# Diagonal of a 2-D prefix sum: engines in program order, six loads queued, the last groups cut in pieces, the last rows folded

## Chip, cores, metric

One core of a Trainium2 chip. The metric is device time in microseconds (us). The profile's span, from the first to the last instruction, is mostly 1.7 to 2 us shorter than the time (in a few runs up to 3.5). In profile lines PE is TensorE, PEld its weight loads, DVE VectorE, ACT ScalarE, POOL GpSimd and SP SyncE (a q behind it is the engine's queue), and L312 is line 312 of the run's kernel.

## The reference

```python
def reference(x):                       # x: float32, (4, 4224, 4224)
    ps = np.cumsum(np.cumsum(x, axis=1), axis=2)
    diag = np.diagonal(ps, axis1=1, axis2=2)
    return np.cumsum(diag, axis=1).astype(np.float32)      # (4, 4224)
```

Element i of the diagonal of `ps` is the sum of the square x[0..i, 0..i]. Its step from i-1 to i is row i left of and on the diagonal plus column i above it. So only row sums up to the diagonal and column sums above it are needed, and then two scans.

## The kernel before

A matrix is cut into 11 groups of 384 rows (3 rows on each of 128 partitions). A group is one DMA that also casts to bf16. TensorE adds the columns right of the group's diagonal block with a vector of ones into one row of `d` in PSUM. VectorE makes the masked diagonal block (`mu`) and, together with ScalarE (`act_sum`), the row sums. At a matrix's end the row sums are transposed into `d` by a matmul with the identity, and two scans run along the 11 rows.

```python
    strips = ctx.enter_context(tc.tile_pool(name="strips", bufs=6))
    ...
    head = last.tile([P, HEAD], FP32, name="head")           # the last 128 rows' last 1056 columns
    nc.sync.dma_start(out=head, in_=x[LB, TB:N, N - HEAD : N])
    ...
    prefetched = {(0, g): load_group(0, g) for g in range(2)}
    ...                                                      # constants
        for g in range(ng):                                  # ng = 11, in the last matrix 10
            strip = prefetched.pop((b, g), None)
            if strip is None:
                strip = load_group(b, g)
            ws = scalar_cols(g)
            for q in range(F):
                nc.vector.scalar_tensor_tensor(out=mu, in0=strip[:, q, lo:hi], ..., accum_out=ru[:, g, q : q + 1])
                columns(g, 0, GW, mu)
                if ws > 0:
                    act_sum(sa[:, g, q : q + 1], strip[:, q, :ws])
            nc.vector.reduce_sum(out=rs[:, g, :], in_=strip[:, :, ws:hi], axis=AX.X)
            for j in range(g + 1, NG):
                for q in range(F):
                    columns(j, 0, GW, strip[:, q, j * GW : (j + 1) * GW])
        ...                                # rows = rs + sa - ru, identity matmuls, scans, carries, y, store
```

In the last matrix the eleventh group is treated apart: 256 rows as pairs (`strip`, four DMAs) and the last 128 rows (`tail`, three DMAs). Their sums follow the scans in the text, but the tile scheduler orders every engine's instructions, so the text's order is not the executed one.

## Time and profile before

| | before |
|---|---|
| time, median of 3 | 674.47 us (674.30 to 674.58) |
| span | 672.8 us |
| bytes read from HBM | 285.47 MB, the input once |
| last full group (group 9 of the last matrix) starts to be worked on | 649.3 us |
| last piece of data landed | 663.3 us |
| final store issued | 670.8 us |

The table is read from its end: between the last data and the end lie 9.5 us, and before that the transfers set the pace. I call the moment when the engines start on the last data of group 9 "L9" all through the text. A strip is the tile of one group, a piece a range of its columns that is loaded by its own DMA, and a crossing is the time from the end of an instruction on one engine to the start of the next on another.

### The profile page before, as it was taken

Reading aid. Unit: us, or ns where it says so; the run is one execution under the profiler, and the core shown is the slowest. Engines: PE = TensorE matmul, PEld = TensorE weight load, DVE = VectorE, ACT = ScalarE, POOL = GpSimd, SP = SyncE. Lnnn points to the kernel's source line nnn. Section 1 sums busy time; section 2 is a strip of 40 time slices with the busy share of each in tenths; the row PEclk is TensorE's granted clock in tenths of the full one; section 3 lists DMA queues with packets and bytes.
Section 4 is the critical chain, followed back from the end, with each engine's and each line's share of the span. In section 5 each row is a group of like instructions: output and inputs, shape, how many; then the busy total and the mean of one; then the engine's idle time right before and its main releaser. Section 6 shows DMA issues by size and latency. Waiting matters only on the chain.

```text
span 672.8 us, 2608 instructions
## 1 busy us (share of the span) xinstructions
PE 232.5 (35%) x852; PEld 91.2 (14%) x852; DVE 259.3 (39%) x370; ACT 153.9 (23%) x249; POOL 31.8 (5%) x67
## 2 busy tenths in 40 slices
PE   0073453211155543321116543232204534344213
PEld 0031111000022211100002211110001211111001
DVE  2033333344543223334563222334555222234458
ACT  0011222233301112223420111223440011123342
POOL 3010000000000000000000000000000000100000
PEclk9997766555577766566557766766555776766655
DMA  9999999999999999999999999999999999999994
GB/s 202 217 215 218 217 217 217 217 217 217 217 219 217 217 218 217 217 217 217 217 217 218 218 217 217 217 215 217 218 217 217 217 217 218 217 217 217 217 201 76
DMA packets 7958, 143.23 MB, mean 213 GB/s; under 512 B 861, under 2 KB 1546, under 8 KB 2442
## 3 DMA queue, kind: packets, MB, share of 16 engines
q0 software_dynamic: 7712, 142.47, 99.0%
q1 hardware_dynamic: 234, 0.61, 0.3%
q8 instruction: 6, 0.10, 0.1%
q14 instruction: 6, 0.05, 0.0%
HBM read 285.47 MB, written 0.07 MB: 424 GB/s over the span
## 4 chain that ended last, share of the span: by engine, by line
another core or an unknown queue 51%; DVE 36%; DMA 11%; issue 1%; POOL 0%; PE 0%; DVEq 0%; POOLq 0%
DVE rs L252 24%; DMA strip<-in_x_dram 11%; DVE mu L240 9%; DVE lrs L334 1%; DVE c L198 1%; DVE c L190 1%; DVE y L281 0%; DVE y L273 0%; DVE tsum L362 0%; POOL strip L60 0%; DVE lc L190 0%; DVE lc L198 0%; PE d_last L156 0%; DVEq L240 0%
## 5 line engine op out<-in xcount | busy, mean ns | idle before, releaser
L165 ACT ACTIVATE dump<-strip 128x192 bf16<-128x192 bf16 (+11 forms) x124 | 141.1, 1138 | 507.7 <-DMA strip<-in_x_dram 505.1
L240 DVE SCALAR_TENSOR_TENSOR mu<-strip,um 128x384 bf16<-128x384 bf16 x129 | 65.5, 554 | 380.9 <-DMA strip<-in_x_dram 380.9
L252 DVE TENSOR_REDUCE rs<-strip 128x3 f32<-128x1152 bf16 (+10 forms) x43 | 169.8, 3950 | 27.5 <-DMA strip<-in_x_dram 27.5
L156 PE MATMUL d<-mu,sel 128*11 128x384 bf16 x129 | 59.2, 476 | 318.8 <-DVE mu L240 318.5
L156 PE MATMUL d<-strip,sel 128*11 128x384 bf16 x630 | 161.9, 431 | 0.0
L156 PEld LDWEIGHTS <-sel 128*11 128x11 bf16 (+1 forms) x794 | 86.7, 109 | 538.8 <-issue 515.2
L60 POOL DMA_DIRECT2D strip<-in_x_dram x43 | 23.0, 535 | 507.5 <-PE d L156 256.7
L156 PE MATMUL d_last<-strip,sel 128*1 128x384 bf16 (+1 forms) x32 | 14.2, 477 | 84.8 <-DMA strip<-in_x_dram 84.8
L165 ACT ACTIVATION_READ_ACCUMULATOR dump<-strip 128x1 f32 x124 | 23.1, 186 | 0.0
L156 PE MATMUL d<-ident,rows 128*11 128x128 f32 (+1 forms) x24 | 5.8, 415 | 19.9 <-DVE sa L219 13.2
L240 DVE DVE_READ_ACCUMULATOR mu<-strip,um 128x1 f32 x129 | 10.5, 82 | 0.0
L156 PEld LDWEIGHTS d<-ident,rows 128*11 128x11 f32 (+1 forms) x24 | 2.7, 128 | 24.0 <-DVE sa L219 15.0
L156 PE MATMUL fin<-wtri,tsum 128*1 128x128 f32 x8 | 2.4, 401 | 6.7 <-DVE tsum L362 3.9
L334 DVE TENSOR_REDUCE lrs<-strip 128x2 f32<-128x1664 bf16 (+2 forms) x3 | 4.4, 1459 | 0.0
L198 DVE TENSOR_TENSOR_SCAN c<-ones_row,c 11x384 f32<-11x384 f32 (+1 forms) x4 | 3.8, 940 | 0.0
L190 DVE TENSOR_TENSOR_SCAN c<-ones_row,d 11x384 f32<-11x384 f32 (+1 forms) x4 | 3.7, 935 | 0.0
L308 POOL DMA_DIRECT2D strip<-in_x_dram x3 | 1.6, 538 | 43.1 <-DMA strip<-in_x_dram 28.5
L362 DVE TENSOR_REDUCE tsum<-strip 128x1 f32<-128x792 bf16 (+2 forms) x3 | 2.9, 952 | 0.0
L156 PE MATMUL d_last<-mu,sel 128*1 128x256 bf16 x2 | 0.8, 396 | 5.5 <-DVE mu L316 5.5
L304 POOL DMA_DIRECT2D strip<-in_x_dram x3 | 2.1, 708 | 6.7 <-DMA strip<-in_x_dram 6.7
L82 POOL TENSOR_SCALAR_AFFINE_SELECT um<-um 128x384 bf16<-128x384 bf16 (+2 forms) x6 | 2.4, 434 | 0.1
L281 DVE TENSOR_TENSOR y<-y,c 11x384 f32<-11x384 f32 (+1 forms) x4 | 2.2, 545 | 0.1
(56 smaller groups left out, 24.1 us busy)
## 6 DMA issues: line engine op xcount, KB each, us to landing
strip<-in_x_dram POOLq DMA_DIRECT2D x43, 3168.0 KB, 81.7
strip<-in_x_dram POOLq DMA_DIRECT2D x1, 832.0 KB, 72.7
strip<-in_x_dram POOLq DMA_DIRECT2D x1, 672.0 KB, 75.2
head<-in_x_dram SPq DMA_DIRECT2D x1, 528.0 KB, 3.8
strip<-in_x_dram POOLq DMA_DIRECT2D x1, 416.0 KB, 69.8
strip<-in_x_dram POOLq DMA_DIRECT2D x1, 396.0 KB, 56.5
strip<-in_x_dram POOLq DMA_DIRECT2D x1, 264.0 KB, 43.1
strip<-in_x_dram POOLq DMA_DIRECT2D x1, 192.0 KB, 69.4
```

The source lines that it names most:

```text
L60: nc.gpsimd.dma_start(out=t, in_=x[b, r0 : r0 + GW, :].rearrange("(p f) w -> p f w", f=F),)
L82: nc.gpsimd.affine_select(out=um, in_=um, compare_op=ALU.is_gt, fill=0.0, base=-q, pattern=[[1, P * f]], channel_multiplier=-f,)
L156: nc.tensor.matmul(o, lhsT=lhsT, rhs=rhs, start=start, stop=False, skip_group_check=True)
L165: nc.scalar.activation(out=dump[:, :w], in_=src, func=ACT.Copy, accum_out=acc)
L190: nc.vector.tensor_tensor_scan(out=c12[:rows, 0, :width], data0=ones_row[:rows, :width], data1=d, initial=init1, op0=ALU.mult, op1=ALU.add,)
L198: nc.vector.tensor_tensor_scan(out=c12[:rows, 1, :width], data0=ones_row[:rows, :width], data1=c12[:rows, 0, :width], initial=init2, op0=A ...
L240: nc.vector.scalar_tensor_tensor(out=mu, in0=strip[:, q, lo:hi], scalar=1.0, in1=um3[q], op0=ALU.mult, op1=ALU.mult, accum_out=ru[:, g, q ...
L252: nc.vector.reduce_sum(out=rs[:, g, :], in_=strip[:, :, ws:hi], axis=AX.X)
L281: nc.vector.tensor_add(out=y[:ng, :], in0=y[:ng, :], in1=c12[:ng, 1, :])
L304: nc.gpsimd.dma_start(out=strip[:, :2, c0:c1], in_=src[:, :, c0:c1])
L334: nc.vector.reduce_sum(out=lrs[:, :, i + 1], in_=strip[:, :2, c0 + ws : c1], axis=AX.X)
L362: nc.vector.reduce_sum(out=tsum[:, k : k + 1], in_=tail[:, 0, c0:c1], axis=AX.X)
```

## The change

The intent: make each engine run in the text's order (`manual_schedule`), so that the writer decides what comes last; queue six loads at once; take work off the end by loading the diagonal part of the last group first (in fp32, at time zero), by cutting groups 8 and 9 of the last matrix in column pieces and the last rows in smaller ones, and by letting TensorE fold 1536 columns of the last rows to 256.

```diff
+    NBUF = 6
+    ctx.enter_context(tc.manual_schedule())
-    head = last.tile([P, HEAD], FP32, name="head")
-    nc.sync.dma_start(out=head, in_=x[LB, TB:N, N - HEAD : N])
+    head_a = last.tile([P, 2, GW], FP32, name="head_a")
+    nc.sync.dma_start(out=head_a, in_=x[LB, T0:TB, T0:N].rearrange("(p f) w -> p f w", f=2))
+    head_b = last.tile([P, HB], FP32, name="head_b")
+    nc.sync.dma_start(out=head_b, in_=x[LB, TB:N, N - HB : N])
-    prefetched = {(0, g): load_group(0, g) for g in range(2)}
+    prefetched = {(0, g): load_group(0, g) for g in range(NBUF)}
...  (three casts of constants go from VectorE to GpSimd)
+    CUTS = {NG - 3: (2176,), NG - 2: (2176, 768)}        # groups 8 and 9 of the last matrix
...  (masked products and row sums of head_a, head_b at the start)
...  (in the loop: column sums first; for a cut group each piece gets a ScalarE and a VectorE sum in `parts`)
-        # ten groups' output y: before everything of the last group, in the text
+        between(b, ng, c12, carry_ps)                      # same place, now a function
-        cuts = [r0, 2176, 832, 0]   (and the diagonal part as its own load)
+        cuts = [(1920, T0), (640, 1920), (0, 640)]
-        tcuts = [N - HEAD, 1584, 528, 0]
+        tcuts = [(2432, N - HB), (1024, 2432), (384, 1024), (0, 384)]
-        (both rows of a pair shared by halves of their columns; four partial sums, four small instructions)
+        for i, (c0, c1) in enumerate(cuts):
+            act_sum(lsa[:, i, 0:1], strip[:, 0, c0:c1])
+            nc.vector.reduce_sum(out=lsa[:, i, 1:2], in_=strip[:, 1, c0:c1], axis=AX.X)
+            for q in range(2):
+                matmul(d_last[:, q : 2 * P : 2], lsa[:, i, q : q + 1], ident)
-        (each partial sum of the last rows: its own weighted matmul into fin)
+        for c0 in range(tcuts[0][0], tcuts[0][1], 2 * P):
+            matmul(fold, ident_h, tail[:, 0, c0 : c0 + 2 * P], start=c0 == tcuts[0][0])
+        nc.vector.reduce_sum(out=tsum[:, 0:1], in_=fold, axis=AX.X)
...  (three more pieces, ScalarE takes 640, 256 and 0 columns of them, VectorE 768, 384, 384)
+        nc.vector.reduce_sum(out=ttot, in_=tsum, axis=AX.X)
+        matmul(fin, ttot, wtri, start=True)
```

## The prediction

> **What bounds the kernel now.** I read the page first (busy table, the 40 slices, the queues), then the chain of waits of the last 40 us, then the timeline of the last 12 us. The page says who is full:
>
> ```profile
> PE 232.5 (35%) x852; PEld 91.2 (14%) x852; DVE 259.3 (39%) x370; ACT 153.9 (23%) x249; POOL 31.8 (5%) x67
> DMA  9999999999999999999999999999999999999994
> q0 software_dynamic: 7712, 142.47, 99.0%
> HBM read 285.47 MB, written 0.07 MB: 424 GB/s over the span
> ```
>
> No engine is above 39% of the 672.8 us span, while the DMA engines are full in 39 of 40 slices. 285.47 MB is the input exactly once (4 x 4224 x 4224 x 4 bytes). A full strip of 384 rows is 6.49 MB and, in the chain, strips release the engines every 14.95 to 14.96 us (95.23, 110.20, 125.15): 434 GB/s. So the body is transfer time and only its two ends can move. The last slice (4) is the end. The chain there, times in us and what ran:
>
> ```profile
> 641.33 7.88 another core or an unknown queue
> ...
> 649.30 0.95 DVE mu L240 x3
> ...
> 650.82 6.07 DVE rs L252
> ...
> 660.17 0.84 DVE c L190
> 661.01 1.45 DVE lrs L334
> ...
> 665.47 0.90 DVE tsum L362
> ```
>
> Up to 649.25 the engines wait for the last full strip (group 9 of the last matrix; call its landing L9). After it VectorE is the chain without a hole. When did the transfers end? The issues with their time to landing, and the issue of the last piece:
>
> ```profile
> strip<-in_x_dram POOLq DMA_DIRECT2D x1, 132.0 KB, 28.8
> 634.53 0.53 POOL L308 DMA_DIRECT2D strip<-in_x_dram  x1 [14.41 <-DMA strip<-in_x_dram]
> ```
>
> 634.53 + 28.8 = 663.3, so all data is there at L9 + 14.1. The span ends at L9 + 23.55, 9.5 us later. What VectorE does in between:
>
> ```profile
> 663.25 0.98 DVE L334 TENSOR_REDUCE lrs<-strip 128x2 f32<-128x832 bf16 x1
> 665.40 0.96 DVE L362 TENSOR_REDUCE tsum<-strip 128x1 f32<-128x792 bf16 x1
> 666.36 1.23 DVE L362 TENSOR_REDUCE tsum<-strip 128x1 f32<-128x1056 bf16 x1
> 667.89 1.00 DVE L190 TENSOR_TENSOR_SCAN lc<-ones_row,lcarry,d_last 1x384 f32<-1x384 f32 x1 [0.30 <-PE d_last L156]
> 668.82 0.67 DVE L362 TENSOR_REDUCE tsum<-strip 128x1 f32<-128x528 bf16 x1
> 669.42 0.99 DVE L198 TENSOR_TENSOR_SCAN lc<-ones_row,lcarry,lc 1x384 f32<-1x384 f32 x1
> 670.51 0.28 DVE L368 TENSOR_TENSOR yl<-fin,lc 1x128 f32<-1x128 f32 x1
> 670.82 0.23 SPq L369 DMA_DIRECT2D out_dram<-yl  x1
> ```
>
> VectorE is about 8 us behind the data: it started group 9's 7.6 us of work only at L9 (649.30 to 656.89). The final store takes 672.8 - 670.82 = 1.98 us. The measured time is 674.47 - 672.8 = 1.67 us above the span.
>
> **What the Trainium skill says.** "DMA: Bandwidth & Descriptors", section "Where 436 GB/s comes from", gives a ceiling of 435.2 GB/s for a core's 16 ports; the 434 GB/s above agrees, so the body cannot get faster. The same page, "Why small descriptors are slow", gives about 3 cycles fixed per packet (at the page's 850 MHz, 3.5 ns). Here: after L9 come 2904 KiB (832+672+416+192+396+264+132), at 217.2 GB/s (the page's usual slice) 13.7 us; they took 14.1, so 0.4 us for 1408 packets on 16 engines (88 each), about 4.5 ns per packet. This agrees roughly. "VectorE: DVE Perf Modes", section "The perf-mode tier table", has tensor_reduce at 1x in every type; the trace has 1.35 us for 1152 elements and 6.15 for 5760, that is 1.042 ns per element + 0.14 us, of which about 0.07 overlaps the next instruction. "ScalarE: Activation LUTs", section "What ACT_TABLE_LOAD costs", has 186 ns + 0.833 ns per element; the trace has 1.80 us for 1920, and with the accumulator read one sum per 0.83 ns x w + 0.32 us.
>
> **The change part by part.**
>
> *Start and body.* The fp32 head is 384 + 128 KiB instead of 528, in 384 small packets instead of 128: by the estimate above under 0.1 us. Six loads are queued at once instead of two. The third strip's load was already queued at 6.01, and the fourth at 39.49, ten us before the third landed (49.8), so no hole existed to close: 0, perhaps 0.5 gained, because the fourth landed 15.5 us after the third. Program order in the body puts VectorE in series at a matrix's end: masked diagonal products 1.55 + largest row sum 6.5 + row sums 0.3 + identity matmuls 1.5 + two scans 1.85 + carries 0.6 + output 1.1 = 13.4 us, under the 14.95 us of a strip, with five more strips queued. 0.
>
> *Cutting groups 8 and 9.* Rows of 4 KB and less in place of 24.7 KB runs: 128 x 3 x (2 + 3) = 1920 packets instead of 256, 104 more per DMA engine, x 4.5 ns = +0.5 us for L9 and all that follows. In return, of group 9 only the last 768 columns are unsummed at L9.
>
> *The end, in us after the new L9.* Arrivals at 212 GB/s (the rate of 650 to 660), 207 KiB per us: strip pieces of 960, 640, 320 KiB at 4.6, 7.7, 9.3; tail pieces of 384, 352, 160, 96 KiB at 11.1, 12.8, 13.6, 14.05.
> 1. Group 9's last piece: VectorE 3 x 384 elements, 1.35 (to 1.4); ScalarE three sums of 384, 3 x 0.64 = 1.9 (to 2.0), the later one. Two small instructions: rows at 2.3.
> 2. Three fp32 identity matmuls, 1.45 as before (657.83 to 659.28): 3.8. Scans from 3.9, 0.86 + 0.94: 5.7. Carry matmuls as in 663.33 to 663.80, and crossing: 6.3.
> 3. Two carry copies 0.17, output multiply 0.4, add 0.47: VectorE free at 7.35. Before it did this at 665.4 - 649.25 = 16.1.
> 4. One row of the pair goes to ScalarE, one to VectorE: 1920, 1280 and 640 elements, one after the other 2.07 + 1.40 + 0.74: 7.35 to 11.6. All three had landed. ScalarE is done with its share at about 10.1.
> 5. One fp32 matmul of two passes and the crossings, 0.65: 12.3. Scans 0.93 + 0.92: 14.15.
> 6. Fold: six bf16 matmuls of 256 columns, 0.21 to 0.32 each from 384 columns in 0.32, start at 12.25: done about 14.0, beside the scans. Copy 0.07, then its sum of 256: 0.5: 14.75.
> 7. Row sums of 768, 384, 384: 0.87 + 0.47 + 0.47: 16.55. Sum of seven 0.2: 16.8. Weighted matmul 0.65 (two passes 0.58 in the trace): 17.45. Add and crossing 0.35: 17.8. Store 1.98: 19.8.
>
> Sum: 23.55 - 19.8 = 3.75 us gained behind L9, 0.6 lost ahead of it: 3.15 us. 674.47 - 3.15 = 671.3.
>
> The fold takes 1536 columns off VectorE for a 256-column sum, some 1.2 us against halving; starting diagonal products at time zero saves 0.8 of products and 0.6 of row sum at the end; the largest share is group 9's 7.6 us brought down to 1.4 behind L9, of which the waits of steps 1, 2 and 5 in program order give much back.
>
> **The rivals.**
> (a) The end becomes limited by transfers. For it: the pieces are sized so. Against: step 4 starts 2.7 us after its data and the chain reaches the last tail piece at 16.1, two us after it lands. If VectorE had nothing else left, landing at 14.05 plus 0.55 + 0.2 + 0.65 + 0.35 + 1.98 would end at 17.8: 669.3. That is the floor.
> (b) The pieces cost more transfer time than I took: 1 us or more, as each also has its own completion. For it: the whole-kernel limit is transfers. Against: the measured 0.4 us for seven pieces with still smaller packets. It would give 672 to 673.
> (c) Program order makes engines wait on each other at matrix ends until loads stop. For it: the buffer of group g can be reused only when the slowest engine has left it. Against: with six buffers the queue is 81.7 us deep (issue to landing of a full strip) for 15 us of work. If a hole of several us did come at each of three matrix ends: 680.
> (d) In program order one instruction of the end blocks VectorE for longer than I reckon (the wait for ScalarE in step 1, or for TensorE in 2 and 5, at the halved clock that the slices show): up to +1 us, 672.3.
>
> **Range and chances.** The middle is the sum, 671.2 with a little for the possible gain at the start. Floor (a) and risk (b) with (d) put eight tenths between 669.6 and 673.0. Two per cent is 13.5 us: only the floor of transfer, 657 us, plus start and end (some 4 us each) could be near a gain of that size, and nothing here reaches it. A loss of that size needs (c).
>
> **What would show it.** L9 (the first instruction on group 9's last piece) should be 649.3 to 650.2; later means (b), earlier means a gain at the start. From there the first scan should begin at +3.9, the first sum of the last pair of rows at +7.35, the one-row scans at +12.3, the final add at +17.5. VectorE should wait at +1.4, at +2.3, at about +5.7 and at +11.6, and nowhere for a transfer after L9. GB/s should stay at 217 until group 8 and be 210 to 216 after it. I am wrong if the DMA row shows a digit below 9 before the last two slices, or if VectorE waits for a transfer among the tail pieces.

## The result and the profile after

| | before | after |
|---|---|---|
| time, median of 4 | 674.49 us | 672.25 us (672.17 to 672.44) |
| span of the profiled run | 672.8 us | 670.5 us |
| L9 | 649.3 us | 650.3 us |
| span's end after L9 | 23.5 us | 20.2 us |

The ratio is 0.9968 (95% interval 0.995 to 0.9985): faster by 2.2 us, 0.3%. Ratios here are the mean time of one kernel's fast runs over that of the other's of the same rounds, so not quite the ratio of the medians quoted.

The page of the changed kernel, DMA row, what each slice moved, the loads' queue, and bytes:

```profile
DMA  9999999999999999999999999999999999999996
GB/s 199 220 218 217 218 218 218 216 218 218 215 218 218 218 217 216 215 216 216 215 216 217 216 218 218 216 216 218 217 216 219 216 218 217 218 216 206 215 212 114
...
q0 software_dynamic: 9296, 142.48, 99.6%
...
HBM read 285.47 MB, written 0.07 MB: 426 GB/s over the span
```

Same bytes, still full in 39 of 40 slices: the body stayed transfer time. The packets grew from 7712 to 9296, mostly as the cut groups have more and shorter runs. The chain of waits around L9 (start, us, what; the view keeps only the longest pieces, so the first one shown is ScalarE's last sum just before L9, and its three sums of 0.62 us behind L9 are left out):

```profile
649.39 0.88 ACT dump L183 x2
652.75 1.47 PE d L173 x6
654.24 0.95 DVE c L216
...
657.98 3.47 DVE lsa L377 x2
661.49 1.45 PE d_last L173 x6
662.96 1.01 DVE lc L216
```

Before, this stretch was VectorE, but for 1.45 us of TensorE (666.41 to 667.87 there). Now the chain passes from engine to engine: ScalarE's last sums, identity matmuls, scans, sums of the last pair, matmuls, scans. VectorE's timeline shows the waits (in brackets, us and for whom):

```profile
650.32 1.35 DVE L332 TENSOR_REDUCE parts<-strip 128x3 f32<-128x1152 bf16 x1 [0.46 <-DMA strip<-in_x_dram]
652.32 0.17 DVE L287 TENSOR_REDUCE rs<-parts 128x3 f32<-128x18 f32 x1 [0.65 <-ACT dump L183]
...
654.24 0.94 DVE L216 TENSOR_TENSOR_SCAN c<-ones_row,d 10x384 f32<-10x384 f32 x1 [1.54 <-PE d L173]
...
656.68 0.15 DVE L360 COPY lcarry<-lcarry_ps 1x2 f32<-1x2 f32 x1 [0.52 <-PE lcarry_ps L173]
...
657.90 4.25 DVE L377 TENSOR_REDUCE lsa<-strip 128x1 f32<-128x1920 bf16 x3
662.96 1.00 DVE L216 TENSOR_TENSOR_SCAN lc<-ones_row,lcarry,d_last 1x384 f32<-1x384 f32 x1 [0.80 <-PE d_last L173]
664.00 1.00 DVE L224 TENSOR_TENSOR_SCAN lc<-ones_row,lcarry,lc 1x384 f32<-1x384 f32 x1
...
665.31 1.85 DVE L404 TENSOR_REDUCE tsum<-strip 128x1 f32<-128x768 bf16 x3
667.26 0.16 DVE L409 TENSOR_REDUCE ttot<-tsum 128x1 f32<-128x7 f32 x1
668.19 0.28 DVE L413 TENSOR_TENSOR yl<-fin,lc 1x128 f32<-1x128 f32 x1 [0.77 <-PE fin L173]
```

After L9 VectorE has only 1.35 us of group 9 left, where it had 7.6. But 4.3 us of waits for other engines came in (0.65 + 1.54 + 0.52 + 0.80 + 0.77). No bracket after 650.32 names a transfer: the end is still a serial order, not data.

### The profile page after: what moved, and what is told of

Same layout as the page of the kernel before. It is cut to its first block, busy times and chain, and to the rows that moved or that the text cites. A ratio compares the mean times of both kernels' runs of the same rounds, so it can differ in the third digit from the quotient of the medians.

```text
span 670.5 us, 2653 instructions
## 1 busy us (share of the span) xinstructions
PE 226.3 (34%) x860; PEld 96.0 (14%) x860; DVE 261.3 (39%) x374; ACT 155.7 (23%) x263; POOL 35.4 (5%) x73
## 3 DMA queue, kind: packets, MB, share of 16 engines
q0 software_dynamic: 9296, 142.48, 99.6%
HBM read 285.47 MB, written 0.07 MB: 426 GB/s over the span
## 4 chain that ended last, share of the span: by engine, by line
another core or an unknown queue 67%; ACT 22%; DMA 7%; DVE 2%; issue 1%; PE 1%; POOL 0%; ACTq 0%; DVEq 0%; POOLq 0%
ACT dump L183 22%; DMA strip<-in_x_dram 7%; DVE lsa L377 1%; DVE tsum L404 0%; PE d L173 0%; PE d_last L173 0%; POOL strip L76 0%; DVE lc L216 0%; DVE lc L224 0%; DVE c L224 0%; DVE c L216 0%; ACTq L183 0%; PE fin L173 0%; DVE y L245 0%
## 5 line engine op out<-in xcount | busy, mean ns | idle before, releaser
L173 PE MATMUL d<-strip,sel 128*11 128x384 bf16 x630 | 174.7, 457 | 346.0 <-DMA strip<-in_x_dram 346.0
L183 ACT ACTIVATE dump<-strip 128x640 bf16<-128x640 bf16 (+14 forms) x131 | 142.3, 1086 | 508.1 <-DMA strip<-in_x_dram 505.3
L173 PEld LDWEIGHTS <-sel 128*11 128x11 bf16 (+1 forms) x792 | 90.2, 114 | 519.1 <-issue 497.1
L324 DVE TENSOR_REDUCE rs<-strip 128x3 f32<-128x1152 bf16 (+10 forms) x41 | 158.2, 3858 | 0.0
L173 PE MATMUL d<-mu,sel 128*11 128x384 bf16 x129 | 38.1, 404 | 40.6 <-DVE mu L312 40.6
L173 PE MATMUL d_last<-strip,sel 128*1 128x384 bf16 x30 | 9.0, 425 | 12.1 <-DMA strip<-in_x_dram 12.1
L332 DVE TENSOR_REDUCE parts<-strip 128x3 f32<-128x3264 bf16 (+2 forms) x3 | 7.3, 2421 | 5.0 <-DMA strip<-in_x_dram 5.0
L324 DVE TENSOR_REDUCE parts<-strip 128x3 f32<-128x2208 bf16 (+1 forms) x2 | 5.3, 2650 | 0.0
L377 DVE TENSOR_REDUCE lsa<-strip 128x1 f32<-128x1920 bf16 (+2 forms) x3 | 4.3, 1465 | 0.0
L173 PE MATMUL d_last<-ident,lsa 128*1 128x128 f32 x12 | 3.0, 406 | 3.3 <-DVE lsa L377 3.0
```

Of the source, the lines that this page charges most:

```text
L173: nc.tensor.matmul(o, lhsT=lhsT, rhs=rhs, start=start, stop=False, skip_group_check=True)
L183: nc.scalar.activation(out=dump[:, :w], in_=src, func=ACT.Copy, accum_out=acc)
L324: nc.vector.reduce_sum(out=rs_at, in_=strip[:, :, ws:hi], axis=AX.X)
L332: nc.vector.reduce_sum(out=parts[:, :, k + 1], in_=strip[:, :, ws:p1], axis=AX.X)
L377: nc.vector.reduce_sum(out=lsa[:, i, 1:2], in_=strip[:, 1, c0:c1], axis=AX.X)
```

## The experiments

Twelve kernels ran in three sets, each set on one chip with its own runs of the kernel before (medians 674.44, 674.50, 674.62). The changed kernel's 672.25 is from other rounds than theirs; the ratios to the kernel before link them.

### Program order taken out of the changed kernel (a1_auto)

```diff
-    ctx.enter_context(tc.manual_schedule())
```

> The changed kernel with the one statement for program order taken out, so that the tile scheduler orders the instructions again. Theory (the gain comes from the smaller pieces and the moved work, program order only keeps them in a good place): 672 to 674.5 us, VectorE in another order after the last full group lands, but the same instructions. Rival (program order is itself the gain; the scheduler would again put row sums in front of the scans): 675 us or more, slower than the kernel before. If it is under 671.5, program order costs time.

Measured: 682.96 us (682.45 to 683.43), ratio 1.0124; the result was correct. My theory fell. The time is in the rival's range (675 or more), but most of it has another reason than the one that the rival gave. VectorE's timeline and the first load that was issued after the six:

```profile
94.86 4.05 DVE L323 TENSOR_REDUCE rs<-strip 128x3 f32<-128x3744 bf16 x1 [11.54 <-DMA strip<-in_x_dram]
98.83 0.55 DVE L311 SCALAR_TENSOR_TENSOR mu<-strip,um 128x384 bf16<-128x384 bf16 x1
```

```profile
101.02 0.60 POOL L75 DMA_DIRECT2D strip<-in_x_dram  x1 [91.93 <-PE d L172]
```

The row sums of all six queued strips came first (20.6, 35.0, 49.96, 64.9, 79.9, 94.9 us), and the first masked product only at 98.8, though the first strip was there at 20. TensorE's column sums queue behind the products (it waited 72.7 us for the first one), so all six buffers stayed taken, no seventh load could be issued until 101, and the DMA share was 0.00 from 95 to 102:

```profile
95.00:100.00 5.00, 0.56 (x2) 0.17 (x2) 5.00 (x7) 3.44 (x6) 0.00 (x0) 0.50 0.00 0
100.00:102.00 2.00, 1.86 (x6) 0.62 (x6) 2.00 (x10) 0.00 (x0) 0.98 (x2) 0.50 0.00 0
```

(Each row is a stretch, its length, then the busy times of TensorE, its weight loads, VectorE, ScalarE and GpSimd, the clock, DMA share and GB/s.) L9 was 659.35, 9.0 us later than with program order. The end behind L9 took 680.6 - 659.35 = 21.25 us, against 20.2: there the row sums of the last pair did come before the scans, as the rival said, but the whole end is only 1.1 of the 10.7 us.

### The same with two loads queued (a5_auto2)

```diff
-    ctx.enter_context(tc.manual_schedule())
-    prefetched = {(0, g): load_group(0, g) for g in range(NBUF)}
+    prefetched = {(0, g): load_group(0, g) for g in range(2)}
```

> Program order taken out as in the run at 682.96 us, but with two loads queued at the start instead of six. In that run the masked products of all six queued strips began only at 98.8 us, after the row sums of all six, and so no buffer came free and the transfers stood still between 95 and 102. Theory (the scheduler puts the masks behind as many strips as loads were issued before them: one more reason for program order once six are queued): products start at 36 to 37 us as in the kernel before, no hole, group 9 lands at 650 to 650.5, 673.3 to 674.2 us. Rival (the hole comes from the head work or anything else of the change): still 680 us or more.

Measured: 673.19 us (673.08 to 673.71), ratio 0.9979.

```profile
35.24 1.95 DVE L323 TENSOR_REDUCE rs<-strip 128x3 f32<-128x1728 bf16 x1 [13.12 <-DMA strip<-in_x_dram]
37.12 0.55 DVE L311 SCALAR_TENSOR_TENSOR mu<-strip,um 128x384 bf16<-128x384 bf16 x1
```

As the theory had it: products behind two strips instead of six, no hole (the time is 0.1 below its range). In these two runs, then, the scheduler put the products behind as many strips as were queued ahead of the masks. This was in the kernel before too (its first product ran at 36.64) and cost nothing there: three loads were out by then and three buffers free. That the scheduler reckons the masks to be late on GpSimd, behind the loads, is my reading of this; I have not seen its reckoning. Behind L9 this run took 671.2 - 650.06 = 21.1 us, again 1.0 more than in program order.

### Two loads queued, in program order (a3_prefetch2)

```diff
-    prefetched = {(0, g): load_group(0, g) for g in range(NBUF)}
+    prefetched = {(0, g): load_group(0, g) for g in range(2)}
```

> The changed kernel with two loads queued at the start instead of six. It asks for the 0.47 us by which the first strip landed later in the changed kernel (20.29 against 19.81). Theory (the head's small packets cost it): no change, first work on strip 0 at 20.2 to 20.4, 672.2 us. Rival (six loads issued at once disturb the start): 19.8 and 671.8 us.

Measured: 672.29 us (672.15 to 672.57), span 670.3. The six loads bring nothing and cost nothing in program order. Six need the order (a1_auto), and the order doesn't need six.

### The kernel before in program order (b1_order)

```diff
+    ctx.enter_context(tc.manual_schedule())
     HEAD = 1056
```

> The kernel before with only the statement for program order added. Theory (program order by itself costs at the end, where the old text puts the scans of ten groups before the last rows' sums and waits at each step): body unchanged, last full group at 649.2 to 649.8, then some 4 to 5 us more on VectorE: 678 to 680 us. Rival (program order by itself is a gain): under 674.

Measured: 679.09 us (678.89 to 679.19), ratio 1.0064. L9 was 649.40, so the body was unchanged and nearly all of the 4.6 us lies behind it (28.0 us against 23.5).

```profile
650.84 6.15 DVE L253 TENSOR_REDUCE rs<-strip 128x3 f32<-128x5760 bf16 x1
...
659.05 0.94 DVE L191 TENSOR_TENSOR_SCAN c<-ones_row,d 10x384 f32<-10x384 f32 x1 [1.54 <-PE d L157]
...
663.91 4.25 DVE L335 TENSOR_REDUCE lrs<-strip 128x2 f32<-128x1664 bf16 x3
```

Program order is no gain by itself: the old text runs 7.6 us of group 9's products and sums, waits, scans, waits, and VectorE starts on the last group only at 662.62. On the new text the order is worth 0.9 us (673.19 to 672.29, both with two loads; spans of 670.9 to 671.2 against 670.1 to 670.3). So of the 2.2 us some 1.3 came with the new text alone, in the scheduler's order.

### Groups 8 and 9 whole (a2_nocuts)

```diff
-    CUTS = {NG - 3: (2176,), NG - 2: (2176, 768)}
+    CUTS = {}
-        if whole:
-            sum_up(0, ng)
+        sum_up(0, ng)
```

> The changed kernel, but groups 8 and 9 of the last matrix are loaded whole again and summed as the others. Theory (cutting costs 0.4 to 0.5 us of transfer and takes 6 us of VectorE off the end): group 9 lands at 649.7 to 650.0 instead of 650.3, VectorE needs 7.6 us after it instead of 1.4, and everything behind it moves: 677 to 678 us. Rival (other waits hide the row sums, as the last pieces land only 14 us later): 673 to 674 us.

Measured: 677.60 us (677.39 to 677.73), ratio 1.0044, in the range that the theory gave.

```profile
649.78 0.56 DVE L312 SCALAR_TENSOR_TENSOR mu<-strip,um 128x384 bf16<-128x384 bf16 x1 [7.98 <-DMA strip<-in_x_dram]
...
651.23 6.15 DVE L324 TENSOR_REDUCE rs<-strip 128x3 f32<-128x5760 bf16 x1
```

The 6.15 us sum stands behind L9 again, and everything after it moves. In program order the cuts are worth 5.3 us (677.60 - 672.29, a3_prefetch2 of the same set): without them the changed kernel is 3.2 us slower than the kernel before, with them 2.2 faster. What they are worth in the scheduler's order was not run, and neither the fold, the smaller pieces of the last rows nor the early diagonal part were taken out one at a time, so their shares stay open. L9 was 0.54 us earlier than in the changed kernel, but 0.23 of that is there already at the second strip (35.01 against 35.24), before any piece: the pieces cost 0.3 us at most by this run.

### One head load in big packets (a4_headbig)

```diff
-    head_a = last.tile([P, 2, GW], FP32, name="head_a")      # and head_b, and their two loads
+    head = last.tile([P, 1024], FP32, name="head")
+    nc.sync.dma_start(out=head, in_=x[LB, 0:P, 0:1024])      # wrong columns on purpose
+    head_a = head[:, 0:768].rearrange("p (f w) -> p f w", f=2)
+    head_b = head[:, 768:1024]
```

> Wrong result on purpose: the two head loads (384 packets of 1.5 and 1 KB) become one load of as many bytes in 128 packets of 4 KB, from other columns of x; the same instructions work on it. Theory (the packets' number costs the start): first work on strip 0 at 19.8, 671.8 us. Rival (it does not; something else moved the start): 20.3 and 672.3 us. In both the second load no longer waits between the strips' big packets, so VectorE's first sums are done by 8 us instead of 21.

Measured: 672.95 us (672.12 to 674.22). The result is wrong by what the edit does. The lowest of four runs is the changed kernel's time, and the profiled run had its first work at 21.98, later than all others; why the runs lie 2.1 us apart I do not know. So the number of packets by itself is not shown to cost anything. What the run did show is what happened to the second head load. Issues of the changed kernel, and below of this one (KB, us to landing):

```profile
head_b<-in_x_dram SPq DMA_DIRECT2D x1, 128.0 KB, 18.9
```

```profile
head<-in_x_dram SPq DMA_DIRECT2D x1, 512.0 KB, 3.6
```

128 KB took 18.9 us, 512 KB 3.6. The Trainium skill, "DMA: Bandwidth & Descriptors", section "Queues, rings and completion order", says that each DMA engine takes turns between queues packet by packet. A strip packet is 25.3 KB (3 x 4224 x 2 bytes), which at 217.2 / 16 = 13.6 GB/s is 1.87 us. `head_b` has 8 packets on each engine, so 8 turns behind a strip packet, 15 us. It was issued behind `head_a`, which landed at 4.5, and landed at 20.4, 15.9 us later: this agrees, if a packet of the profile is one turn (the page's packets hold several descriptors, 9 to 17 as a rule). In program order VectorE then stands at `head_b` until 20.48, which is when the first strip lands anyway, so it costs nothing here.

### Two loads and one head load (a6_start)

The edits of a3_prefetch2 and a4_headbig together; wrong result.

> Wrong result on purpose: the changed kernel with one 4 KB-packet head load and two loads queued, the start of the kernel before. Theory (the start lost 0.25 to 0.5 us through both together, each alone did not show): second strip's first work at 34.8 instead of 35.0 to 35.2, 671.9 us. Rival (the start scatters from run to run and has no cause in the change): 672.2 us, with runs spread as in the run with one head load and six queued (672.1 to 674.2).

Measured: 671.83 us (671.59 to 673.18), median as the theory had it, but the profile did not bear it out: the second strip's first work came at 35.15, in the range of the others. Its gain lies between the second strip and L9 (614.50 us, against 615.08 in the changed kernel), where the edit does nothing that I know of. Inconclusive. The start of the changed kernel is 0.2 to 0.5 us longer than in the one profile of before, and the cause is open.

### Ten groups' output moved behind the pair's sums (c1_between)

```diff
-        between(b, ng, c12, carry_ps)
         lsa = last.tile([P, 3, 2], FP32, name="lsa")
         ...
+        between(b, ng, c12, carry_ps)
         lc = last.tile([1, 2, GW], FP32, name="lc")
```

> The changed kernel with the output of groups 0 to 9 of the last matrix (two carry copies, multiply, add: 1.2 us of VectorE) moved from before the last pair's row sums to after them, where VectorE waits 0.80 us for TensorE. Theory (VectorE's serial order after group 9 sets the end): 0.8 us less, 671.4 to 671.6. Rival (the last transfers set the end): no change, 672.2.

Measured: 671.35 us (671.18 to 671.43), ratio 0.995, spans 669.3 to 669.5 against 670.3 to 670.5.

```profile
661.95 0.99 DVE L216 TENSOR_TENSOR_SCAN lc<-ones_row,lcarry,d_last 1x384 f32<-1x384 f32 x1
```

The bracket is gone: 0.9 us less, the wait of 0.80 filled with work that had to be done anyway (one of the two carry copies stayed in its place, by the edit). This is what program order allows: the writer can put work into a known wait.

### The last rows shared otherwise (c2_tail)

```diff
-        for c0 in range(tcuts[0][0], tcuts[0][1], 2 * P):    # fold: first piece
+        for c0, c1 in tcuts[:2]:                              # fold: first two pieces
+            for lo in range(c0, c1, 2 * P): ...
-        (VectorE 768 + 384 + 384 columns, ScalarE 640 + 256)
+        act_sum(tsum[:, 1:2], tail[:, 0, tcuts[2][0] : tcuts[2][1]])         # third piece, ScalarE
+        nc.vector.reduce_sum(out=tsum[:, 2:3], in_=tail[:, 0, 0:384], ...)   # fourth, VectorE
+        nc.vector.reduce_sum(out=tsum[:, 0:1], in_=fold, axis=AX.X)
```

> The changed kernel with the last rows' sums shared otherwise: the fold on TensorE takes the second tail piece too (1408 more columns), ScalarE the third whole, VectorE only the fourth (384) and the fold's 256. VectorE's work behind the one-row scans falls from 0.40 + 1.85 us to about 0.9. Theory (VectorE is the chain there): the fold ends at 665.4 at the latest, the sum of parts starts at 666.0 instead of 667.3: 671.0 us. Rival (the fold at the halved clock becomes the bound): 671.8 or more.

Measured: 670.71 us (670.35 to 671.66), ratio 0.9942; spans 668.5 to 668.9. The gain in the span is 1.6 us, more than the 1.25 that I had reckoned.

```profile
662.53 2.63 PE L173 MATMUL fold<-strip,ident_h 128*128 128x256 bf16 x12
665.20 0.42 DVE L404 TENSOR_REDUCE tsum<-fold 128x1 f32<-128x256 f32 x1
```

TensorE's twelve folds ended at 665.16, just before VectorE came to them, so the rival fell. The sum of parts started 15.74 us after L9 instead of 16.94: 1.2 us, about what I had reckoned (666.0 for 667.3). What goes beyond it is 0.2 us in the final weighted matmul (0.38 us instead of 0.59; the granted clock was 1.00 in its stretch of the profile, 666 to 667, and 0.67 in that of the changed kernel, 667 to 668), and the rest lies before L9.

### Both moves, and two variants (c3_both, c4_both_bal, c5_g9only)

```diff
 c3_both:      the edits of c1_between and c2_tail
 c4_both_bal:  and in group 9's last piece
-                ws = p0 + (p1 - p0) // 2
+                ws = p0 + (p1 - p0) // (2 if p0 else 3) // 32 * 32
 c5_g9only:    and
-    CUTS = {NG - 3: (2176,), NG - 2: (2176, 768)}
+    CUTS = {NG - 2: (2176, 768)}
```

> The two moves together: the output of groups 0 to 9 after the last pair's sums, and the last rows' sums shared with TensorE and ScalarE. Theory (the serial order was the chain until now; the last piece of data, some 14.1 us after group 9 in these profiles, becomes the bound): not the sum of both gains (2.4 us) but less, VectorE waits a little for the last piece, 670.0 to 670.3 us. Rival (still VectorE alone): the full sum, 669.8 or less.

> As the run with both moves, and of group 9's last 768 columns ScalarE sums 256 instead of 384, so that VectorE does not wait 0.65 us for it. The rows of group 9 are ready 0.4 us sooner. Theory (the last piece is the bound now): no gain, within 0.15 us of the run with both moves. Rival (VectorE's chain is still the bound): 0.4 us less.

> As the run before it, but group 8 is loaded whole again and only group 9 in pieces; VectorE has 15 us for group 8 in any case. Theory (each packet more costs about 4.5 ns on its DMA engine, and the last piece is the bound): 768 packets become 128, 40 fewer on each engine, 0.2 us less than the run before it: 669.8 to 670.0 us. Rival (the cut of group 8 is needed to spread the row sums, or costs nothing): no gain, or slower.

Measured: 670.12 us (c3_both), 669.98 (c4_both_bal), 669.80 (c5_g9only); ratios 0.9936, 0.9938, 0.9931, all three results correct. In c3_both:

```profile
664.08 0.55 DVE L401 TENSOR_REDUCE tsum<-strip 128x1 f32<-128x384 bf16 x1 [0.29 <-DMA strip<-in_x_dram]
```

Now VectorE waits for the last piece of data. The gains of the two moves (0.9 and 1.6) do not add up, as expected, and the balance in c4_both_bal brings nothing: the spans are 668.1 to 668.3 and 668.0 to 668.2. The spans of c5_g9only are 667.9 to 668.2, so its 0.18 us in the median lies outside the span and is not a gain from fewer packets; that theory is not confirmed (the last piece was first worked on 629.06 us after the second strip, 629.04 in c4_both_bal). Cutting group 8 is not needed, though. These kernels beat both the kernel before and the changed one, by 0.6 to 0.7% and 0.3 to 0.4%. What remains behind the last piece of data, from 664.08 to the span's end at 668.1, is 4.0 us: its own sum and the fold's, the total, a matmul, an add and the store.

## Why the prediction was right, and where its sizes were off

The time, 672.25, lies in the upper part of the range of 669.6 to 673.0. The direction and the mechanism held. The size did not quite: 3.3 us forecast, 2.2 measured. Its steps against the trace, in us after L9:

| step | predicted | measured |
|---|---|---|
| L9 itself | 649.85 (649.25 + 0.6) | 650.32 |
| 1. rows of group 9 ready | 2.3 | 2.37 |
| 2. ten groups' scans start; carry copied | 3.9; 6.3 | 3.92; 6.36 |
| 3. VectorE free for the last pair | 7.35 | 7.58 |
| 4. and 5. one-row scans start | 12.3 | 12.64 |
| VectorE free for the last rows | 14.15 | 14.61 |
| 6. fold's sum done | 14.75 | 14.99 |
| 7. sum of parts starts; final add starts | 16.55; 17.5 | 16.94; 17.87 |
| end of the span | 19.8 | 20.18 |

**The mis-sized terms.** The first is "under 0.1 us" and "0, perhaps 0.5 gained" for the start. In the ten profiles with two head loads (with two or six strips queued) the second strip was first worked on between 34.97 and 35.24, against 34.77 before: 0.2 to 0.5 us lost, 0.47 in the profile of the changed kernel. Which part of the start does it is open, and so is how much of it is the change: the four profiles with one head load scatter more (34.77 before, 34.46 in b1_order, 35.15 in a6_start, 36.92 in a4_headbig). One thing does go with two head loads: the instruction that issues the first one takes 0.64 us instead of 0.40. With one load again (a6_start, 0.39) the second strip came no earlier, though. The second is the chain behind L9, 0.4 us too short: step 3 by 0.17, steps 4 and 5 up to the scans by 0.11, their two scans by 0.12 and step 7's row sums by 0.15, while step 6 was 0.22 too long. For step 3 and the scans the trace tells why. I took the spacing of these instructions from the kernel before, where the scheduler had put something else between two that depend on each other. There a scan and the sum behind it started 0.93 us apart (667.89 and 668.82 in the prediction's lines). In program order the second scan follows the first directly and starts 1.04 us after it (662.96, 664.00). The scans of ten rows do the same (0.97 apart here, 0.86 from the scan to an unrelated sum before). Each such pair costs about 0.1 us more. The third lies outside the span: the time is 1.94 us above it in the profiled run, and 1.9 to 2.0 in the three others, against the 1.67 that I added. The kernel before and b1_order, with the old text, lie 1.66 to 1.77 above it in all their runs, the kernels with the new text 1.67 to 3.48. So it goes with the new text and not with the order alone; its cause I can't show.

**The term for the pieces**, +0.5, is not confirmed. From the second strip to L9 the kernels with whole groups took 614.53 (before), 614.94 (b1_order) and 614.77 us (a2_nocuts), and the ten profiles with pieces and no hole 614.50 to 615.15: the cost is lost in this scatter. c5_g9only, with 40 packets fewer on each engine, showed none.

**Readings that were off.** The 434 GB/s is what was read from HBM in fp32. Written to SBUF in bf16 is half of it, the 217 of the slices, so it is not measured at the 16 ports of which the quoted 435.2 speaks, and that the body cannot get faster is not shown by it. And the fold's "some 1.2 us against halving" is its gain against VectorE summing all 1536 columns (1.6 us against 0.4); against halving it is about 0.5 (0.96 us for 792 columns before, 0.40 for the fold's sum now).

**The rivals.** (a) was not the case in the changed kernel, where no wait of VectorE after L9 is for a transfer, and came true once both moves were made (c3_both, 0.29 us). (b) and (d) had named the time that was measured (672 to 673, and 672.3), but by mechanisms that the runs do not show. By the sign that the prediction had set (L9 later than 650.2), 650.32 speaks for (b), and so does the slice of 206 GB/s at the end (210 to 216 was named); yet 0.47 us was lost before any piece, and the pieces cost at most a few tenths. (c), a hole in the transfers, did not occur in program order. (d), waits of VectorE for others, happened at the four places that were named and before the final add, where step 7 has the matmul: 4.3 us in all, nearly all of it already in the sum; the further loss in this chain is the 0.4 us above, not 1 us.

**What I had not seen.** I gave the program order no size, only waits that it brings. It is the term with most in it: 4.6 us lost on the old text, 0.9 gained on the new, and 10.7 gained where six loads are queued (682.96 to 672.25). The last is not in the difference between the two kernels, but it tells why program order and six loads are one choice.

## What to carry to other kernels

When transfers fill the body, look for the time between the last data and the end, and follow one engine's order there instruction by instruction; then check whether any bracket in it names a transfer, since as long as none does, moving work into the waits or to other engines still pays (here some 2 us more, until one did). Cutting the last loads so that only a little of them is unsummed when they land was worth 5.3 us in program order, for a transfer cost too small to be seen here. An instruction order that is harmless with two loads queued can hold all buffers when six are queued: after raising the number of loads in flight, look at when the first buffer is released.

## What the Trainium skill lacked or had wrong

- "DMA: Bandwidth & Descriptors", "Where 436 GB/s comes from": its warning says that for transfers between HBM and SBUF the HBM side, about 358 GB/s, binds. The page's own "Measured" (425 GB/s, the pair's other core idle) does not fit that for one core alone, and neither do these runs, of a program on one core: 285.47 MB read at 424 and 426 GB/s over the whole span, a strip at 434.
- "DMA: Bandwidth & Descriptors", "Measured": its rule of 1 MiB and more per DMA for 75% of peak does not say what holds for smaller ones back to back in a queue. Here pieces of 96 to 960 KB after L9 ran at 211 GB/s (written side) against 217 for the whole strips.
- The same page, "Queues, rings and completion order": it has the turns by packet, but not what they do to a small load: 128 KB in 8 packets per engine took 18.9 us beside packets of 25 KB, 512 KB issued alone before them 3.6 us.
- "VectorE: DVE Perf Modes", "The DRAIN you can't avoid": it measured, on eight copies, that a semaphore between neighbours costs nothing extra. Here two scans of which the second needs the first start 1.04 us apart; with a second instruction that needs nothing of it, 0.93. Whether the semaphore or the need itself does it, the traces do not show.
- No page says what the order of instructions that a scheduler chooses does to buffers: with six loads queued it kept all six buffers until 101 us, and L9 came 9.0 us later than in program order.
